# A decoder trunk's attention: rotating and transposing the queries one block ahead

## The chip, the cores and the metric

The kernel runs on one core of a Trainium2 chip. Its time is the device time of one execution in microseconds (us). Shown are the median, the lowest and the highest of three runs, and one further execution that the hardware profiler recorded; the rows of the trace come from that one.

## The reference

The reference is a trunk of two layers over one sequence of 512 tokens of width 1024. Each layer has a mixer of three head groups, which read one combined projection of the normalised input, and after it an MLP:

```python
for l in range(DEPTH):
    h = _rmsnorm(x, norm_mix_g[l])
    z = h @ w_in[l]
    q, k, v, qi, ki, wi, u5, z_ssd, xbc, dt_raw = _split(z, IN_SIZES)
    attn_out = _dsa_mixer(q, k, v, qi, ki, wi, ...)   # sparse attention, 8 heads of 64
    s5_out = _s5_mixer(u5, ...)                       # 16 groups of a complex diagonal scan
    ssd_out = _ssd_mixer(z_ssd, xbc, dt_raw, ...)     # Mamba-2, 4 heads of 64, chunks of 128
    mix = jnp.concatenate([attn_out, s5_out, ssd_out], axis=-1) @ w_out[l]
    x = x + mix
    h2 = _rmsnorm(x, norm_mlp_g[l])
    x = x + (jax.nn.relu(h2 @ w_up[l]) ** 2) @ w_down[l]
```

The attention goes over four blocks of 128 queries. Eight small index heads score every earlier token, and the 128 best of each query are kept. The queries and keys are normalised and the first 16 of their 64 elements are rotated by position; then comes softmax over the kept keys, and the sum of the values.

## The kernel before

**Streams and their merge.** One call of `mixers(l)` (L1382) does the mixer of a layer, as several Python generators: `trunk_in` (the input projection with its evacuations), `keys` (keys, then the index scores of blocks 1 to 3), `select` (the masks), `attention`, `recurrent` for S5 and for SSD, three parts of `out_proj`, and in layer 0 the tables of S5. `merge` (L1172) runs them in one another's gaps: each stream has a clock, the stream with the lowest clock takes its next step, and the number that the step yields is added to its clock. A step that yields None has to wait for another stream. The numbers are costs times a pace: `pace["q"]` is 3.616 in the first mixer and 3.741 in the second, so that the `pace["q"] * 2.5` after a query step is 9.04 and 9.35 units; a softmax of block b yields `pace["att"] * (0.4 + 0.25 * b)`, with 1.702 and 1.652. This fixes in which order the instructions are traced. The tile framework then orders them for each engine by priority and dependence; a stream's priority can be shifted (attention: 300 and 1000).

**Tiles.** Nearly all large tiles come from `g()` (L243), whose tag "g" has 52 buffers of 128 x 512 floats: weights have their own, but the queries, the head copies, the logits and their exponentials, the evacuated projections `xb` and `z` and, through `h()` (L247), SSD's tiles are all of it. Small tiles come from `s()` (L261) with a tag each. The PSUM banks are two pools, "m" and "a", of four banks each.

**Attention.** `attention` (L1341) waits until all four query blocks and the keys are there, computes the scale of each query head, and goes over the blocks. The step that this document calls a query step is in two parts. `rope_q` (L1033) rotates a block's queries with four VectorE operations on 16 elements of each head (L1038 to L1041), with a scratch tile `rsw` of its own tag. `transpose_heads` (L1071) then turns the eight heads so that the head's dimension lies on the partitions, in two halves of four heads each:

```python
t = self.g([P, 4, 2, 64], F32R, name="hhl")
nc.scalar.activation(t[:, :, 0], x, AF.Copy)                                    # L1078
nc.vector.tensor_tensor(t[:, :, 1], x, t[:, :, 0].bitcast(F32), ALU.subtract)   # L1079
p = self.ps(self.bank["hT"], (P, 4, P), name="hTp")
for i in range(4): nc.tensor.transpose(p[:, i], ...)                            # L1082
o = self.g([P, 4, P], F32R, name="hT")
nc.scalar.activation(o, p, AF.Copy)                                             # L1084
```

When the block's mask is there (block 0 has a constant one; `topk_masks` (L1116) makes the others, with the last write at L1126), `attend` (L1128) does the block: for each of eight heads the logits `lg` (TensorE, L1091), their masked maximum into `pe` (VectorE, L1143) and the exponential (ScalarE, L1144); the scaling by the reciprocal of the sum (L1151 and L1153); then for each block of keys the transposes `pTp` (L1159), their evacuation `pT` (ScalarE, L1161) and the product with the values into `po` (L1164); and the split of the result into `mh` and `ml` (L1168, L1169).

**Work beside it.** `trunk_in` evacuates the projections: `xb` at L1246 and `z` at L1249, both on VectorE. `ssd` (L828) makes from `xb` the convolution `cv` (L880 to L887) and the tiles `CT` (L893, L894), and then, chunk by chunk, the products `ssdT`, `ssds`, `ssdy` (L943, L945) with the VectorE work between them. `out_proj` (L1396) multiplies each group's `mh` and `ml` with the output weights as soon as they are complete (L458 to L460, which are the lines of every weight product).

Of the kernel before, what the change touches and what calls it, by code (L numbers as in the profile page):

```python
# [22 lines left out]
NB = S // P  # L23
# [197 lines left out]
class Net:  # L221
# [1119 lines left out]
    def attention(self, l, r):  # L1341
        nc = self.nc
        while len(r.get("q", ())) < NB or "K" not in r:
            yield None
        yield self.start["att"]
        q, rt = r["q"], self.rt
        qms = self.s([P, NB, NH], tag="qms", bufs=1)
        qrs = self.s([P, NB, NH], tag="qrs", bufs=1)
        for b in range(NB):
            self.head_ms(qms[:, b], q[b], NH)  # L1350
            yield self.pace["q"] * 0.7
        self.rsqrt(qrs.rearrange("p b h -> p (b h)"), qms.rearrange("p b h -> p (b h)"), NB * NH)
        nc.vector.tensor_scalar(qrs, qrs, -ATT_SCALE, None, ALU.mult)
        ah = [self.g(dt=F32R, name="mh") for _ in range(4)]
        al = [self.g(dt=F32R, name="ml") for _ in range(4)]
        for b in range(NB):
            self.rope_q(q[b], *rt[2][b])
            qT = self.transpose_heads(q[b])
            yield self.pace["q"] * 2.5
            while b not in r["mask"]:  # L1360
                yield None
            yield from self.attend(b, qT, r["K"], r["mask"][b], qrs[:, b], ah, al)
        for i in range(4):
            self.tap(f"at_{l}_{i}", ah[i].bitcast(F32)); self.tap(f"atl_{l}_{i}", al[i].bitcast(F32))
        r["mix"]["att"] = list(zip(ah, al))
# [252 lines left out]
```

## Time and profile before

| | us |
|---|---|
| median of 3 runs | 1325.63 |
| lowest and highest | 1324.28, 1325.82 |
| the profiled execution | 1325.5 |
| its span, first to last instruction | 1323.7 |
| TensorE busy (matmuls) | 1219.9 (92%) |
| VectorE busy | 888.7 (67%) |
| ScalarE busy | 548.9 (41%) |
| mean granted TensorE clock | 0.966 |

Engines are called PE (TensorE; PEld is its weight load), DVE (VectorE), ACT (ScalarE), POOL (GpSimd) and SP (SyncE). The profile gives the busy time of each, the idle time before an instruction with the instruction that ended it, and timelines; L1143 is a line of the kernel, and `pe<-lg,isc,qrs` names what is written and what is read. A row of a timeline has the start, the duration, the engine, the line and the operation; equal neighbours are one row with their count, such as x4. The first mixer's attention lies at 120 to 301 us of the span, the second's at 825 to 932 us; the MLPs fill most of the rest.

### The profile page before, as it was taken

Reading aid. Unit: us, or ns where it says so; the run is one execution under the profiler, and the core shown is the slowest. Engines: PE = TensorE matmul, PEld = TensorE weight load, DVE = VectorE, ACT = ScalarE, POOL = GpSimd, SP = SyncE. Lnnn points to the kernel's source line nnn. Section 1 sums busy time; section 2 is a strip of 40 time slices with the busy share of each in tenths; the row PEclk is TensorE's granted clock in tenths of the full one; section 3 lists DMA queues with packets and bytes.
Section 4 is the critical chain, followed back from the end, with each engine's and each line's share of the span. In section 5 each row is a group of like instructions: output and inputs, shape, how many; then the busy total and the mean of one; then the engine's idle time right before and its main releaser. Section 6 shows DMA issues by size and latency. Waiting matters only on the chain.

```text
span 1323.7 us, 17056 instructions
## 1 busy us (share of the span) xinstructions
PE 1219.9 (92%) x5708; PEld 979.0 (74%) x5708; DVE 888.7 (67%) x2024; ACT 548.9 (41%) x1128; POOL 172.8 (13%) x302
## 2 busy tenths in 40 slices
PE   5678967889999999999999988968999999999998
PEld 5566755458888888888888767744788888888887
DVE  5998999857877755554573699975475445445443
ACT  4245543663543533534443334455254243242331
POOL 2386100000599100000100000000000000000000
PEclk9789978899999999999999989978999999999999
DMA  5122320002467776686654634300323333333332
GB/s 190 40 80 65 81 81 9 24 1 71 130 196 253 230 252 217 218 266 199 211 171 145 204 120 129 112 17 1 111 89 103 96 96 96 96 99 99 97 111 80
DMA packets 139688, 161.64 MB, mean 122 GB/s; under 512 B 18768, under 2 KB 107600, under 8 KB 139600
## 3 DMA queue, kind: packets, MB, share of 16 engines
q1 hardware_dynamic: 139600, 160.55, 38.8%
q8 instruction: 45, 0.74, 0.2%
q14 instruction: 43, 0.35, 0.1%
HBM read 128.29 MB, written 31.03 MB: 120 GB/s over the span
## 4 chain that ended last, share of the span: by engine, by line
PE 74%; DVE 19%; ACT 4%; issue 2%; DMA 0%; SPq 0%; ACTq 0%; DVEq 0%
PE pm L458 21%; PE pm L460 21%; PE pm L459 21%; PE po L1164 3%; DVE isc L1123 2%; DVE mx L1122 2%; PE pTp L1159 1%; DVE isc L1112 1%; DVE pe L1143 1%; DVE cv L883 1%; ACT pe L1144 1%; PE hTp L1082 1%; DVE wlo L192 1%; DVE hhl L1079 0%; PE bct L428 0%
## 5 line engine op out<-in xcount | busy, mean ns | idle before, releaser
L192 DVE TENSOR_TENSOR wlo<-wraw,whi 128x512 fp32r<-128x512 f32 (+1 forms) x312 | 225.6, 726 | 230.5 <-ACT whi L191 224.2
L191 ACT ACTIVATE whi<-wraw 128x512 fp32r<-128x512 f32 (+1 forms) x312 | 194.5, 625 | 378.5 <-PE pm L459 252.0
L458 PE MATMUL pm<-xh,whi 128*128 128x512 f32 x640 | 252.7, 396 | 3.8 <-ACT q L1260 3.3
L460 PE MATMUL pm<-xh,wlo 128*128 128x512 f32 x640 | 250.9, 393 | 1.2 <-DVE wlo L192 1.2
L459 PE MATMUL pm<-xl,whi 128*128 128x512 f32 x640 | 251.4, 393 | 0.0
L458 PE MATMUL pm<-uh,whi 128*128 128x512 f32 x512 | 199.7, 390 | 0.0
L459 PE MATMUL pm<-ul,whi 128*128 128x512 f32 x512 | 199.2, 389 | 0.0
L460 PE MATMUL pm<-uh,wlo 128*128 128x512 f32 x512 | 198.9, 389 | 0.0
L458 PEld LDWEIGHTS pm<-xh,whi 128*128 128x128 f32 x640 | 121.2, 190 | 31.5 <-ACT q L1260 4.0
L460 PEld LDWEIGHTS pm<-xh,wlo 128*128 128x128 f32 x640 | 121.2, 189 | 27.2 <-DVE wlo L192 2.0
L459 PEld LDWEIGHTS pm<-xl,whi 128*128 128x128 f32 x640 | 121.3, 190 | 24.5 <-issue 0.2
L458 PEld LDWEIGHTS pm<-uh,whi 128*128 128x128 f32 x512 | 96.1, 188 | 20.0 <-issue 0.2
L460 PEld LDWEIGHTS pm<-uh,wlo 128*128 128x128 f32 x512 | 96.1, 188 | 19.9
L459 PEld LDWEIGHTS pm<-ul,whi 128*128 128x128 f32 x512 | 96.2, 188 | 19.9
L458 PE MATMUL pm<-whi,xh 128*128 128x512 f32 (+1 forms) x176 | 67.6, 386 | 13.8 <-ACT xh L392 12.8
L460 PE MATMUL pm<-whi,xl 128*128 128x512 f32 (+1 forms) x176 | 66.9, 382 | 1.1 <-DVE xl L394 1.1
L459 PE MATMUL pm<-wlo,xh 128*128 128x512 f32 (+1 forms) x176 | 67.5, 383 | 0.1
L1444 DVE TENSOR_TENSOR ul<-ur,uh 128x512 fp32r<-128x512 f32 x64 | 48.7, 762 | 20.7 <-ACT uh L1443 20.4
L1442 DVE SCALAR_TENSOR_TENSOR ur<-pm,ur 128x512 f32<-128x512 f32 x64 | 43.9, 685 | 26.5 <-ACT ur L1439 26.5
L1450 DVE TENSOR_TENSOR sq<-pm,r2b 128x512 f32<-128x512 f32 x64 | 44.1, 689 | 22.4 <-PE pm L460 22.3
L1443 ACT ACTIVATE uh<-ur 128x512 fp32r<-128x512 f32 x64 | 40.0, 625 | 30.5 <-DVE ur L1442 30.5
L1123 DVE MATCH_REPLACE8 isc<-mx,isc 128x256 f32<-128x256 f32 (+2 forms) x96 | 52.0, 546 | 0.0
(345 smaller groups left out, 1940.3 us busy)
## 6 DMA issues: line engine op xcount, KB each, us to landing
wraw<-in_w_up_dram SPq DMA_DIRECT2D x128, 256.0 KB, 2.8
wraw<-in_w_down_dram SPq DMA_DIRECT2D x128, 256.0 KB, 2.8
st<-shi SPq DMA_DIRECT2D x48, 256.0 KB, 2.8
st<-slo SPq DMA_DIRECT2D x48, 256.0 KB, 3.4
wlo<-st SPq DMA_DIRECT2D x48, 256.0 KB, 2.9
whi<-st SPq DMA_DIRECT2D x48, 256.0 KB, 2.8
wraw<-in_w_in_dram SPq DMA_DIRECT2D x32, 256.0 KB, 2.8
sraw<-in_w_in_dram SPq DMA_DIRECT2D x32, 256.0 KB, 3.4
```

The lines of the kernel that those rows point to most:

```text
L191: nc.scalar.activation(hi, raw, AF.Copy)
L192: nc.vector.tensor_tensor(lo, raw, hi.bitcast(F32), ALU.subtract)
L458: nc.tensor.matmul(p, lh, rh, start=first, stop=False)
L459: nc.tensor.matmul(p, lh, rl, start=False, stop=False)
L460: nc.tensor.matmul(p, ll, rh, start=False, stop=last)
L1122: v.max(m8, acc)
L1123: v.match_replace(acc, m8, acc, SENT)
L1164: nc.tensor.matmul(po[g_ * 64:g_ * 64 + 64], self.vt[:, kb, g_], pts[g_], start=kb == 0, stop=kb == b)
L1442: v.scalar_tensor_tensor(r, p, 0.0, r, ALU.max, ALU.mult)
L1443: nc.scalar.activation(h, r, AF.Copy)
L1444: v.tensor_tensor(lo, r, h.bitcast(F32), ALU.subtract)
L1450: v.tensor_tensor(t, d[1], rb, ALU.mult)
```

## The change

The loop over the blocks rotates and transposes two blocks ahead of the first attention, and then always one block ahead:

```diff
         al = [self.g(dt=F32R, name="ml") for _ in range(4)]
+        turned = {}
         for b in range(NB):
-            self.rope_q(q[b], *rt[2][b])
-            qT = self.transpose_heads(q[b])
-            yield self.pace["q"] * 2.5
+
+            for i in range(b, min(b + (2 if True else 1), NB)):
+                if i not in turned:
+                    self.rope_q(q[i], *rt[2][i])
+                    turned[i] = self.transpose_heads(q[i])
+                    yield self.pace["q"] * 2.5
+            qT = turned[b]
             while b not in r["mask"]:
                 yield None
             yield from self.attend(b, qT, r["K"], r["mask"][b], qrs[:, b], ah, al)
```

With T for a query step and A for an attention, the order in the code was T0 A0 T1 A1 T2 A2 T3 A3 and is now T0 T1 A0 T2 A1 T3 A2 A3. The pause in the merge after each step goes with it. It holds in both mixers.

## Rows read from the trace of the kernel before

**Rows 1.** The page: busy time, share of the span and instructions of each engine.
```profile
PE 1219.9 (92%) x5708; PEld 979.0 (74%) x5708; DVE 888.7 (67%) x2024; ACT 548.9 (41%) x1128; POOL 172.8 (13%) x302
```

**Rows 2.** Windows: length, busy us of PE, PEld, DVE, ACT, POOL; PE clock, DMA share, GB/s.
```profile
120.00:160.00 40.00, 38.27 (x184) 29.07 (x182) 39.87 (x123) 24.40 (x54) 6.11 (x10) 1.00 0.25 65
...
216.00:301.00 85.00, 72.67 (x362) 47.70 (x362) 64.33 (x180) 50.16 (x135) 0.00 (x0) 0.92 0.04 13
838.00:931.00 93.00, 75.76 (x376) 50.22 (x376) 64.52 (x191) 52.71 (x147) 0.00 (x0) 0.89 0.10 33
```

**Rows 3.** PE's waits, 216 to 301 us, then 838 to 931: us in all, times, longest.
```profile
PE hTp L1082 <- DVE hhl L1079: 3.0, 3, 1.3
...
PE ssds L929 <- DVE CT L894: 4.2, 1, 4.2
PE ssdT L916 <- DVE cv L887: 3.5, 1, 3.5
```

**Rows 4.** Timeline of ACT in mixer 1, block 1's query step.
```profile
220.57 0.63 ACT L191 ACTIVATE whi<-wraw 128x512 fp32r<-128x512 f32 x1 [6.46 <-PE pm L459]
...
226.65 0.40 ACT L1078 ACTIVATE hhl<-q 128x256 fp32r<-128x256 f32 x1
...
230.62 0.60 ACT L1084 ACTIVATE hT<-hTp 128x512 fp32r<-128x512 f32 x1 [1.27 <-PE hTp L1082]
```

**Rows 5.** Timeline of DVE in mixer 1, 214 to 232 us.
```profile
214.25 1.28 DVE L1249 SCALAR_TENSOR_TENSOR z<-pm,rb 128x512 f32<-128x512 f32 x2
...
223.00 0.69 DVE L894 SCALAR_TENSOR_TENSOR CT<-cth,cv 64x512 f32<-64x512 f32 x1
...
231.93 0.47 DVE L1143 CUSTOM_DVE_ANT_0 pe<-lg,isc,qrs 128x256 f32<-128x256 f32 x1
```

**Rows 6.** Timelines of ACT and DVE in mixer 1, block 3.
```profile
267.74 0.42 ACT L1078 ACTIVATE hhl<-q 128x256 fp32r<-128x256 f32 x1
...
270.39 0.42 DVE L1126 TENSOR_SCALAR isc<-isc 128x512 f32<-128x512 f32 x1
...
272.92 0.75 DVE L1143 CUSTOM_DVE_ANT_0 pe<-lg,isc,qrs 128x512 f32<-128x512 f32 x1
```

**Rows 7.** Timelines of ACT and DVE in mixer 2, block 3.
```profile
899.42 0.42 ACT L1078 ACTIVATE hhl<-q 128x256 fp32r<-128x256 f32 x1
...
906.58 0.74 DVE L1143 CUSTOM_DVE_ANT_0 pe<-lg,isc,qrs 128x512 f32<-128x512 f32 x1
```

**Rows 8.** Timeline of DVE in mixer 1, the last operation of the rotations.
```profile
130.92 0.28 DVE L1041 TENSOR_TENSOR q<-q,rsw 128x128 f32<-128x128 f32 x1
...
137.16 0.28 DVE L1041 TENSOR_TENSOR q<-q,rsw 128x128 f32<-128x128 f32 x1
```

**Rows 9.** Timelines of PE and DVE in mixer 2: the xb product's end, its first evacuation.
```profile
842.93 0.47 PE L460 MATMUL pm<-xh,wlo 128*128 128x512 f32 x1
...
863.77 0.68 DVE L1246 TENSOR_TENSOR xb<-pm,rb 128x512 f32<-128x512 f32 x1
```

**Rows 10.** Timeline of DVE in mixer 1, the last softmax of block 0.
```profile
187.32 0.36 DVE L1143 CUSTOM_DVE_ANT_0 pe<-lg,cons,qrs 128x128 f32<-128x128 f32 x1
187.59 0.10 DVE L1143 DVE_READ_ACCUMULATOR2_ANT nmax<- 128x1 f32 x1
```

**Rows 11.** Timelines of ACT and DVE in mixer 2, block 0 to block 1's first copy.
```profile
833.05 0.42 ACT L1078 ACTIVATE hhl<-q 128x256 fp32r<-128x256 f32 x1 [3.15 <-DVE q L1041]
...
838.73 0.35 DVE L1143 CUSTOM_DVE_ANT_0 pe<-lg,cons,qrs 128x128 f32<-128x128 f32 x1
...
850.98 0.41 ACT L1078 ACTIVATE hhl<-q 128x256 fp32r<-128x256 f32 x1
```

**Rows 12.** Timeline of PE in mixer 1: SSD's last product and the next projection.
```profile
298.08 0.38 PE L945 MATMUL ssdy<-cs,prev 128*64 128x128 f32 x2
298.39 0.74 PE L458 MATMUL pm<-mh,whi 128*128 128x512 f32 x2
```

## The prediction

> **What bounds the kernel now.** I read the page's busy table first. TensorE (PE) is busy for 92% of the span [rows 1], so time can be won only where PE stands idle. The windows show where that is. From 216 to 301 us (the attention stretch of mixer 1) PE is busy 72.67 of 85 us; from 838 to 931 us (the same stretch of mixer 2) 75.76 of 93 us [rows 2]. So 12.3 and 17.2 us of PE idle lie where the four attention blocks run one after another, and 29.6 us bounds any gain there. VectorE (DVE) is not full there: 64.3 of 85 and 64.5 of 93 us. In 120 to 160 us, where the first query step runs, PE has 38.27 of 40 us and DVE 39.87: nothing is to be had there.
>
> Next I read PE's waits in these two stretches. In mixer 1 the transposes wait 3.0 us in three places for DVE's half of the step that the change moves. In mixer 2 the two longest waits are for other work: 4.2 us for SSD's CT and 3.5 us for its convolution [rows 3].
>
> Then I followed one query step from its first copy to the first softmax, block 1 of mixer 1: first head copy at 226.65, second transposed copy (hT) at 230.62, first softmax at 231.93 [rows 4, 5]. That is a gap of 5.3 us in which attention makes no softmax. Block 3 has 5.2 us of it in mixer 1 (267.74 to 272.92) and 7.2 us in mixer 2 (899.42 to 906.58) [rows 6, 7]. These gaps are what the change aims at.
>
> But why does the step come so late? The rotation of all four blocks is done soon after 137.16 us [rows 8] (the first and the last of four stand there). Block 1's query has been ready since then, yet its head copy starts at 226.65, although ScalarE (ACT) stood idle for 6.46 us just before 220.57 [rows 4]. Neither data nor engine is missing. What holds it, as I read the code and the trace together: tiles with the tag "g" are first written in the order in which the code allocates them, so a tile that is late holds every later one. The rotation's scratch tile has its own tag and went early; the head copies are "g" tiles and did not. The same is seen in mixer 2: PE ended the xb product at 843.4, and its evacuation, a "g" tile again, came at 863.77 [rows 9]. I argue from this order in all that follows.
>
> **The change, part by part.** It adds and removes no instruction, and moves no DMA: per block four small DVE operations and, twice, an ACT copy (0.40 us), a DVE subtraction, four transposes and an ACT evacuation (0.60 us) [rows 4] move. No queue of SP or POOL is passed. The order was T0 A0 T1 A1 T2 A2 T3 A3 (T a query step, A an attention); it becomes T0 T1 A0 T2 A1 T3 A2 A3. So if tiles go in the code's order, a step still stands between A0 and A1 and between A1 and A2, only it serves the block after next. Only the gap between A2 and A3 goes, and one step more stands ahead of A0. The pause after each step (9.04 and 9.35 units of the merge's clock) moves too: A0, A1 and A2 are traced that much later against the other streams.
>
> *Mixer 1, T1 ahead of A0:* near 135 to 144 us, beside weight products that fill PE (38.27 of 40). Cost 0; without that cover 4.6 us, first copy to the end of the second hT (226.65 to 231.22) [rows 4].
>
> *Mixer 1, A0 traced later:* by the pace constants A0 now comes after the z product's evacuation (214.25) and after SSD's CT (to 223.69) [rows 5]. Today its softmaxes are long done: the last is at 187.32 [rows 10]. They leave a stretch in which DVE is nearly full, so CT comes about eight softmaxes (0.36 + 0.10 us) or 3.7 us earlier. A0 itself, first softmax to the next head copy, takes 12.25 us in mixer 2 (838.73 to 850.98) [rows 11]. Then 4.0 us to the second hT [rows 4]: 223.7 - 3.7 + 12.25 + 4.0 = 236.2 against 231.93, +4.3. Bounds: -1 if A0 stays where it is, +8 if CT does not come earlier. I take +4.3, by its own rows.
>
> *Mixer 1, A1 to A2:* T3 stands where T2 stood, but A2's first logits do not read it. At most the last hop goes (230.62 to 231.93, 1.3 us): -1.
>
> *Mixer 1, A2 to A3:* -5.2. But mask 3 is final only at 270.39 + 0.42 = 270.81, and A3 starts at 272.92 [rows 6]. With 4.3 - 1 - 5.2 = -1.9 it just fits; half a microsecond for a place in DVE's order leaves **-1.6** (range -5 to +5, the low end if the mask search finishes earlier too).
>
> *Mixer 2, T1 ahead of A0:* PE has products to do then, but attention's chain sets this stretch's end, so I count the step in full: +4.6 (0 to 5.7, the whole step 0 there, 833.05 to 838.73 [rows 11]).
>
> *Mixer 2, xb against A1:* A1 is traced later, so xb's evacuation and the convolution come ahead of about half of A1. That feeds SSD earlier, and the waits of 3.5 and 4.2 us [rows 3] can shrink. Bounds -7.7 (both go) and +4.6 (they push A1 back by as much as a query step); nearest to the waits that are seen, and only in part: -2.
>
> *Mixer 2, last hops twice:* -2. *A2 to A3:* the gap is 7.2 us, but the same instructions take 5.2 in mixer 1; the other 2 are SSD's and stay: -5.2. Mixer 2: 4.6 - 2 - 2 - 5.2 = **-4.6**.
>
> Sum -6.2 against the profiled execution's 1325.5 us (span 1323.7 and 1.8 around it; the median of the runs is 1325.63, so no correction): **1319.3 us**. A no-change result is all within 0.2%, 2.7 us, about what can be told apart here.
>
> **A rule that speaks against it.** What the rows show: the gap repeats at each block, with a free DVE. The Trainium skill, page Perfetto Trace Analysis, section Optimization Strategy, says that the same gap repeating on the engine that should be busy can mean that too few buffers are there for the next tile. By that rule four more live tiles of hhl and hT per block would make the gaps longer. The rows speak for an order rather than a shortage: the rotation, in a tag of its own, went ahead at once, and "g" has 52 buffers, of which I count at most 39 live from the code. No row here shows the occupancy itself.
>
> **Rivals.**
> (a) *Nothing changes.* SSD's output chain ends with attention's: its last product is at 298.08, and the next projection begins at 298.39 [rows 12]. The change doesn't move SSD's chain, and four steps stand in the code as before. For it: that row. Against it: SSD waits in the same queues, so a shorter attention lets it through. 1325.5.
> (b) *Slower.* The order holds A0 and A1 behind SSD's start. Mixer 1 takes its upper bound, +8 - 1 - 5.2 = +1.8; mixer 2 has xb at its upper bound, 4.6 + 4.6 - 2 - 5.2 = +2.0: 1329.3. It decides if A1's first softmax in mixer 1 is later than about 237. For it: CT's end at 223.69 with nothing of A0 done. Against: PE is idle there, and A0 could go faster than in mixer 2.
> (c) *Buffers run short*, the repeated gap being a shortage: each of the four remaining steps between blocks costs another round of 4.6 us instead of saving 1: 18.4 less the 5.2 won back between A2 and A3 is 13.2, so 1338.7.
> (d) *The order doesn't hold*, and all steps slip away beside other work: six gaps of 5.2 us and more, bounded by 29.6 us of PE idle; with half of that, -15: 1310.5. For it: this is what the data dependences allow. Against: the late head copies and the late evacuation [rows 4, 9].
>
> **How the numbers follow.** Forecast 0.45, (a) 0.20, (b) 0.20, (c) 0.05, (d) 0.10. The forecast's own range is 1313 to 1326, so some of its share falls within 0.2%. Faster: 0.38 of the forecast and (d), 0.48. Same: 0.07 of the forecast and (a), 0.27. Slower: (b) and (c), 0.25. The range takes in (d) and (b), 1309.5 to 1331, and leaves out (c) and the far ends.
>
> **What would show it.** Right: the first copy of block 1 near 135 us in mixer 1; head copies of block 2 still only after A0's last evacuation; no head copy between A2 and A3; A3's first softmax near 271 us, right behind its mask; in mixer 2 xb's evacuation before A1 ends, and PE's waits for the convolution and CT smaller. Wrong: if block 2's copies come right behind block 1's, the order doesn't hold and (d) is on; if A1 starts later than 237 us, (b); if A3 starts earlier but the projection still begins near 298.4, (a).

## The result, and the profile after

The changed kernel takes 1341.43 us (median of 4 runs, 1339.46 to 1342.22) against 1325.62 us of the kernel before, measured beside it: a ratio of 1.0124, with a 95% interval of 1.0111 to 1.0136. It is 1.2% slower, some 16 us, where I had forecast 1319.3 us. The profiled execution has a span of 1339.7 us at a mean granted clock of 0.961, against 1323.7 us at 0.966.

The profile's first table says that no work was added: PE has 5708 matmuls as before, is busy for 1224.0 us, against 1219.9 [rows 1], and its share falls to 91%.

```profile
PE 1224.0 (91%) x5708; PEld 980.9 (73%) x5708; DVE 891.8 (67%) x2024; ACT 550.6 (41%) x1128; POOL 176.1 (13%) x302
```

The loss is idle time of PE in the two attention stretches. These are the windows after that answer to the two stretches of [rows 2]; each is 7 to 9 us longer than it was.

```profile
216.00:310.00 94.00, 69.61 (x340) 43.61 (x338) 63.56 (x194) 52.57 (x148) 0.00 (x0) 0.85 0.04 12
847.00:947.00 100.00, 78.55 (x378) 51.41 (x377) 65.28 (x192) 52.55 (x147) 0.00 (x0) 0.85 0.11 31
```

PE is idle 24.4 us of the first and 21.5 us of the second, against 12.3 and 17.2 us before [rows 2]. To give each mixer its share, I take two rows of ACT that mark the same places in every kernel: the first evacuation of the queries (L1260), which comes before anything that the change touches, and the first evacuation of the last block's result (L1168). First the kernel before, then the changed one:

```profile
123.09 0.68 ACT L1260 ACTIVATE q<-pm,rstd 128x512 f32<-128x512 f32 x1
...
297.62 0.28 ACT L1168 ACTIVATE mh<-po 128x128 fp32r<-128x128 f32 x1 [0.64 <-PE po L1164]
...
825.43 0.66 ACT L1260 ACTIVATE q<-pm,rstd 128x512 f32<-128x512 f32 x1
...
931.37 0.28 ACT L1168 ACTIVATE mh<-po 128x128 fp32r<-128x128 f32 x1 [0.65 <-PE po L1164]
```

```profile
121.41 0.68 ACT L1260 ACTIVATE q<-pm,rstd 128x512 f32<-128x512 f32 x1
...
306.50 0.28 ACT L1168 ACTIVATE mh<-po 128x128 fp32r<-128x128 f32 x1 [0.64 <-PE po L1164]
...
834.64 0.67 ACT L1260 ACTIVATE q<-pm,rstd 128x512 f32<-128x512 f32 x1
...
947.31 0.28 ACT L1168 ACTIVATE mh<-po 128x128 fp32r<-128x128 f32 x1 [0.65 <-PE po L1164]
```

Mixer 1 went from 174.5 to 185.1 us, mixer 2 from 105.9 to 112.7 us. That is +10.6 and +6.7; with 1.7 us less ahead of the first row it is nearly the 16.0 us of the spans. One such length from one execution is good to some 2 us: in the six kernels of this document that have mixer 1 as it was, the one before among them, it lies between 174.4 and 176.7.

**Mixer 1 after.** Timelines of ACT (the head copies and hT) and of DVE (the rest), to be held against [rows 4, 5, 6, 10]:

```profile
217.21 0.69 DVE L894 SCALAR_TENSOR_TENSOR CT<-cth,cv 64x512 f32<-64x512 f32 x1
217.91 0.35 DVE L1143 CUSTOM_DVE_ANT_0 pe<-lg,cons,qrs 128x128 f32<-128x128 f32 x1
...
233.89 0.41 ACT L1078 ACTIVATE hhl<-q 128x256 fp32r<-128x256 f32 x1
...
239.91 0.60 ACT L1084 ACTIVATE hT<-hTp 128x512 fp32r<-128x512 f32 x1 [2.34 <-PE hTp L1082]
...
240.98 0.48 DVE L1143 CUSTOM_DVE_ANT_0 pe<-lg,isc,qrs 128x256 f32<-128x256 f32 x1
...
253.89 0.42 DVE L1126 TENSOR_SCALAR isc<-isc 128x512 f32<-128x512 f32 x1
...
279.44 0.74 DVE L1143 CUSTOM_DVE_ANT_0 pe<-lg,isc,qrs 128x512 f32<-128x512 f32 x1
```

Block 1's step is early (142.59), as the change says. But A0, whose softmaxes used to be done by 187.7 us [rows 10], begins only at 217.91, in the very slot behind CT; A1 begins 9 us late, and block 2's step before it takes 6.0 us from copy to hT instead of 4.0. The search for mask 3, in exchange, ends at 254.3 instead of 270.8 us [rows 6].

Two things are different in that step. DVE has a piece of the search (L1122) right ahead of its half of the first copies (L1079), and PE's clock is lower: four transposes take 1.1 instead of 0.6 us. Two rows of the step after; then the window of block 1's step before and that of the step after, with the length, the busy time of PE, PEld, DVE, ACT and POOL, and PE's granted clock:

```profile
234.46 0.68 DVE L1122 MAX8 mx<-isc 128x8 f32<-128x512 f32 x1
235.06 0.41 DVE L1079 TENSOR_TENSOR hhl<-q,hhl 128x256 fp32r<-128x256 f32 x1
```

```profile
226.60:231.20 4.60, 4.08 (x30) 3.55 (x28) 4.42 (x10) 1.93 (x6) 0.00 (x0) 1.00 0.12 39
...
233.90:240.50 6.60, 2.85 (x12) 2.46 (x13) 6.06 (x14) 1.89 (x5) 0.00 (x0) 0.50 0.11 38
```

**Mixer 2 after.** Timelines of DVE, with ACT's first evacuation of A2's result at 918.89:

```profile
871.42 0.48 DVE L1143 CUSTOM_DVE_ANT_0 pe<-lg,isc,qrs 128x256 f32<-128x256 f32 x1
...
871.83 0.69 DVE L1246 TENSOR_TENSOR xb<-pm,rb 128x512 f32<-128x512 f32 x1
...
882.05 0.35 DVE L1143 CUSTOM_DVE_ANT_0 pe<-lg,isc,qrs 128x256 f32<-128x256 f32 x1
...
898.50 0.62 DVE L1143 CUSTOM_DVE_ANT_0 pe<-lg,isc,qrs 128x384 f32<-128x384 f32 x1
...
918.89 0.28 ACT L1168 ACTIVATE mh<-po 128x128 fp32r<-128x128 f32 x1 [0.42 <-PE po L1164]
...
919.41 0.74 DVE L1143 CUSTOM_DVE_ANT_0 pe<-lg,isc,qrs 128x512 f32<-128x512 f32 x1
...
931.92 0.75 DVE L1143 CUSTOM_DVE_ANT_0 pe<-lg,isc,qrs 128x512 f32<-128x512 f32 x1
```

A1 is cut in two: after its fourth softmax (871.42) DVE does xb and the convolution, and the fifth comes at 882.05. The gap from A2 to A3 is gone (918.89 to 919.41), yet A3's eight softmaxes now need 12.5 us. PE's waits after, in 216 to 310 us and in 847 to 947 us:

```profile
PE hTp L1082 <- DVE hhl L1079: 12.1, 4, 5.2
...
PE ssdT L916 <- DVE cv L887: 5.1, 1, 5.1
PE ssdy L943 <- DVE dec L932: 4.5, 1, 4.5
...
PE ssds L929 <- DVE CT L894: 0.2, 1, 0.2
```

The wait for CT is all but gone (0.2 instead of 4.2 us [rows 3]). But the wait for the convolution has grown from 3.5 to 5.1 us, the wait for SSD's decay from 2.7 to 4.5 us, and PE waits 4.0 us, ending at 882.56, for the softmaxes of A1's second half.

### The profile page after: what moved, and what is told of

The parts are those of the page before. It is cut to its first block, busy times and chain, and to the rows that moved or that the text cites. A ratio compares the mean times of both kernels' runs of the same rounds, so it can differ in the third digit from the quotient of the medians.

```text
span 1339.7 us, 17040 instructions
## 1 busy us (share of the span) xinstructions
PE 1224.0 (91%) x5708; PEld 980.9 (73%) x5708; DVE 891.8 (67%) x2024; ACT 550.6 (41%) x1128; POOL 176.1 (13%) x302
## 4 chain that ended last, share of the span: by engine, by line
PE 74%; DVE 17%; ACT 4%; issue 2%; DMA 1%; POOL 0%; SPq 0%; ACTq 0%; DVEq 0%
PE pm L458 21%; PE pm L460 21%; PE pm L459 21%; PE po L1164 3%; DVE isc L1123 2%; DVE mx L1122 1%; PE pTp L1159 1%; DVE isc L1112 1%; ACT pe L1144 1%; DVE cv L883 1%; PE hTp L1082 1%; DVE pe L1143 1%; DMA wraw<-in_w_in_dram 1%; DVE wlo L192 1%; PE s5st L690 1%
## 5 line engine op out<-in xcount | busy, mean ns | idle before, releaser
L192 DVE TENSOR_TENSOR wlo<-wraw,whi 128x512 fp32r<-128x512 f32 (+1 forms) x312 | 228.4, 734 | 225.5 <-ACT whi L191 221.8
L1455 DVE TENSOR_TENSOR sq<-pm,r2b 128x512 f32<-128x512 f32 x64 | 44.1, 689 | 22.2 <-PE pm L460 21.9
L458 PE MATMUL pm<-mh,whi 128*128 128x512 f32 x128 | 50.9, 401 | 1.6 <-ACT mh L820 1.6
```

The lines of the kernel that those rows point to most:

```text
L192: nc.vector.tensor_tensor(lo, raw, hi.bitcast(F32), ALU.subtract)
L458: nc.tensor.matmul(p, lh, rh, start=first, stop=False)
L1455: v.tensor_tensor(t, d[1], rb, ALU.mult)
```

## The experiments

The change has two parts that can be told apart: the **order** of the steps, and the **pauses** that went with them and set where the merge puts each attention. Below, T and A are query steps and attentions as in the description of the change, and the lengths of the mixers are taken as above.

### Order alone, pauses alone, one mixer alone

*The order alone*: every block has one pause, at the place of before.

```diff
-            for i in range(b, min(b + (2 if True else 1), NB)):
+            for i in range(b, min(b + 2, NB)):
                 if i not in turned:
                     self.rope_q(q[i], *rt[2][i])
                     turned[i] = self.transpose_heads(q[i])
-                    yield self.pace["q"] * 2.5
+            yield self.pace["q"] * 2.5
             qT = turned[b]
```

> The query steps stand one block ahead, as in the changed kernel, but each block has its one pause where the kernel before has it, so that every attention is traced at the merge's clock of before. Theory P (place): the loss comes from the pauses, which put attention later against the other streams; then this one is at 1319 to 1329 us, A0's first softmax in mixer 1 is back near 145 to 150 us, and mixer 1 ends within 2 us of before. Theory S (step): the moved steps themselves cost it, by the tiles and banks that they take ahead of the next attention; then it stays at 1335 us or more, with A1 of mixer 1 still starting 5 us or more late.

*The pauses alone*: the kernel before with

```diff
-            yield self.pace["q"] * 2.5
+            for _ in range((2, 1, 1, 0)[b]):
+                yield self.pace["q"] * 2.5
```

> The query steps stand where the kernel before has them, right ahead of their own block; only the pauses are those of the changed kernel (two ahead of A0, one ahead of A1 and A2, none ahead of A3). P: 1335 to 1346 us, A0's first softmax in mixer 1 near 218 us as in the changed kernel. S: 1322 to 1330 us.

*One mixer alone*: in the changed kernel `2 if True else 1` became `2 if l == 0 else 1`, and then `2 if l == 1 else 1`.

> The change in mixer 1 alone. By the offsets of the two traces mixer 1 accounts for 9 us of the 16 and mixer 2 for 7: 1333 to 1336 us if the two are independent. Rival: mixer 2's loss is only a consequence of mixer 1's shift; then this is near 1341 us and the change in mixer 2 alone near 1326 us.

> The change in mixer 2 alone. Independent: 1331 to 1334 us, with the convolution of xb between the softmaxes of A1 and a PE wait for SSD's decay (dec) of over 4 us near A3. Rival: near 1326 us.

Measured, beside the kernel before on the same chip (1325.05 us):

| | us | ratio (95%) | mixer 1 | mixer 2 |
|---|---|---|---|---|
| before (profile above) | | | 174.5 | 105.9 |
| the change (profile above) | 1341.43 | 1.0124 (1.0111 to 1.0136) | 185.1 | 112.7 |
| order alone | 1331.93 | 1.0058 (1.0040 to 1.0076) | 174.5 | 114.6 |
| pauses alone | 1336.29 | 1.0091 (1.0070 to 1.0112) | 183.7 | 106.6 |
| mixer 1 alone | 1334.12 | 1.0073 (1.0055 to 1.0092) | 183.9 | 105.9 |
| mixer 2 alone | 1329.93 | 1.0044 (1.0028 to 1.0059) | 174.4 | 112.3 |

The rows of the first two experiments behind this table, with A0's first softmax in mixer 1 for the order alone; that one first, then mixer 1 of the pauses alone (its mixer 2 goes from 834.95 to 941.59):

```profile
121.64 0.68 ACT L1260 ACTIVATE q<-pm,rstd 128x512 f32<-128x512 f32 x1
...
147.91 0.34 DVE L1143 CUSTOM_DVE_ANT_0 pe<-lg,cons,qrs 128x128 f32<-128x128 f32 x1
...
296.09 0.28 ACT L1168 ACTIVATE mh<-po 128x128 fp32r<-128x128 f32 x1 [0.64 <-PE po L1164]
...
822.97 0.68 ACT L1260 ACTIVATE q<-pm,rstd 128x512 f32<-128x512 f32 x1
...
937.60 0.28 ACT L1168 ACTIVATE mh<-po 128x128 fp32r<-128x128 f32 x1 [0.64 <-PE po L1164]
```

```profile
122.86 0.68 ACT L1260 ACTIVATE q<-pm,rstd 128x512 f32<-128x512 f32 x1
...
306.57 0.28 ACT L1168 ACTIVATE mh<-po 128x128 fp32r<-128x128 f32 x1 [0.64 <-PE po L1164]
```

The order alone lies between the ranges of the two theories, and the pauses alone in that of P. So neither theory holds for the whole kernel; each holds for one mixer. In mixer 1 the loss is the pauses: with the order alone A0 is back at 147.91 and the mixer is as long as before, with the pauses alone it has +9.2 of the +10.6 us, and A0 begins at 217.90. In mixer 2 it is the order: +8.7 us alone, while the pauses alone do +0.7. (Both together do +6.7; that the pauses give 2 us back beside the order is no more than the lengths can tell.) The two mixers are nearly independent: each changed alone has the length that it has in the changed kernel, within 1.2 us, and the two times add up to 14 of the 16 us. Mixer 2 alone came out somewhat below its expectation, with the wait for the decay that it named (4.5 us).

### Mixer 1: is it A0 alone?

One pause more ahead of A0 and one less ahead of A1, in mixer 1 alone: `(2, 0, 1, 1)[b]` pauses instead of one each.

> Order of the steps as in the kernel before; in mixer 1 alone one pause more stands ahead of A0 and one less ahead of A1, so that only A0 is traced later (behind z and CT) and A1 to A3 stay at their old places in the merge. Theory F: mixer 1's whole loss is that A0 falls behind z and CT: A0's first softmax near 218 us, A1's near 240, mixer 1 ends 7 to 10 us late, 1331 to 1336 us. Rival: it needs the later pauses too; then mixer 1 ends within 3 us of before, 1322 to 1328 us.

It took 1327.38 us, a ratio of 1.0023 (1.0008 to 1.0038).

```profile
122.25 0.68 ACT L1260 ACTIVATE q<-pm,rstd 128x512 f32<-128x512 f32 x1
...
301.84 0.28 ACT L1168 ACTIVATE mh<-po 128x128 fp32r<-128x128 f32 x1 [0.65 <-PE po L1164]
```

A0 went where expected (217.53), but the mixer is 179.6 us long, +5.1 in this trace, and the time is only 2.5 us longer, which is within the rival's range. So A0's fall behind CT is half of what the pauses alone cost, or less (5.1 of 9.2 us by the traces, 2.5 of 11.2 by the times), and theory F, that it is all of it, was wrong. What the run with all the pauses has beyond this one is that A1 and A2 too are traced one pause later; they do the rest.

### Mixer 2: which moved step costs?

In mixer 2 only, with pauses as before, I moved one step at a time. *First*: T0 T1 A0 A1 T2 A2 T3 A3. *Last*: T0 A0 T1 A1 T2 T3 A2 A3. The diff is that of *first*; in *last* the four entries are (0,), (1,), (2, 3) and ().

```diff
-            for i in range(b, min(b + (2 if True else 1), NB)):
-                if i not in turned:
...
+            for i in (((0, 1), (), (2,), (3,))[b] if l else (b,)):
+                self.rope_q(q[i], *rt[2][i])
+                turned[i] = self.transpose_heads(q[i])
+            yield self.pace["q"] * 2.5
+            qT = turned[b]
```

> Mixer 2 only, pauses as in the kernel before: block 1's query step is moved ahead of A0, blocks 2 and 3 stay right ahead of their own attention (T0 T1 A0 A1 T2 A2 T3 A3). So as many steps stand ahead of xb's evacuation as before. Theory D (displacement): what the moved steps cost in mixer 2 is that one step more stands ahead of xb and SSD; then A0 starts 4 to 5 us late, the gap of A0 to A1 gives that back, xb is within 1.5 us of its place and the time is within 3 us of before (1322 to 1328). Rival: the step ahead of A0 costs by itself, since A0 then runs beside more of the output product; then xb and the end are 4 us late or more, 1329 or more.

> Mixer 2 only, pauses as before: only block 3's query step is moved, from ahead of A3 to ahead of A2 (T0 A0 T1 A1 T2 T3 A2 A3). My prediction's sum says +4.6 for the step and -5.2 for the gap: 1324 to 1326 us. Theory G (the gap of A2 to A3 is filled by SSD's work, which is taken back in A3): A3 starts near its old place or up to 2 us early against the mixer's start, and the mixer ends 2 to 5 us late: 1327 to 1331 us.

*First* took 1321.41 us against 1324.12, a ratio of 0.9991 (0.9970 to 1.0011): no difference that can be told. Its ten runs lie between 1319.1 and 1328.9, and the profiled one, at 1320.9, is among the short ones. DVE's rows, behind the first query evacuation at 824.61:

```profile
842.74 0.34 DVE L1143 CUSTOM_DVE_ANT_0 pe<-lg,cons,qrs 128x128 f32<-128x128 f32 x1
...
855.96 0.48 DVE L1143 CUSTOM_DVE_ANT_0 pe<-lg,isc,qrs 128x256 f32<-128x256 f32 x1
```

A0 starts 18.1 us behind that row instead of 13.3 (+4.8, the step); A1 31.4 instead of 30.8, and xb (862.67) 38.1 instead of 38.3 us. The gap that lost its step gave nearly all of it back, as theory D has it. In this kernel a step ahead of A0 did no harm where the next gap had none.

*Last* took 1327.2 us, 1.0017 (1.0008 to 1.0027), where my prediction's sum would have it at 1324 to 1326 and theory G at 1327 to 1331. A3 starts 81.3 us after the first row, as it did (81.2), and then the mixer ends 3.1 us late, as theory G has it. Why does A3 take longer? PE's timeline in the gap and in A3, first of the kernel before, then of *last*: SSD's `ssdT`, SSD's `ssdy` behind six of the logits, and the last of A3's logits.

```profile
901.73 0.52 PE L916 MATMUL ssdT<-cons,cv 128*128 128x128 f32 x3
...
911.50 0.45 PE L943 MATMUL ssdy<-dec,xd 128*64 128x128 f32 x4 [2.72 <-DVE dec L932]
...
914.31 0.63 PE L1091 MATMUL lg<-kl,hT 128*128 128x512 f32 x1
```

```profile
907.83 0.27 PE L916 MATMUL ssdT<-cons,cv 128*128 128x128 f32 x1
...
914.88 0.70 PE L943 MATMUL ssdy<-dec,xd 128*64 128x128 f32 x4 [3.88 <-DVE dec L932]
...
919.12 0.63 PE L1091 MATMUL lg<-kl,hT 128*128 128x512 f32 x1
```

In the kernel before, PE does the first products of SSD's next chunk (`ssdT`) while the query step fills the gap ahead of A3. Without the gap they stand among A3's logits, which begin at 906.54, and what is behind them comes later. A3's softmaxes take 12.4 us from first to last instead of 8.4. Of these 4.0 us, 1.2 are the longer wait for the decay (3.88 instead of 2.72 us), 1.4 lie behind it (4.2 instead of 2.8 us to the last logits, as all of `ssdy` stands there ahead of them and not a part), and the other 1.4 ahead of it, where the products of SSD's chunk are. That two logits stand behind `ssdy` and run at the lower clock (0.63 us) is no difference: they do so in the kernel before too.

### Does A3 wait for these two logits?

To take them from behind `ssdy` I put `ssdy` and `st` of mixer 2 into the other PSUM pool (`"dy": "m", "dst": "m"`), once with the last step moved and once in the kernel before.

> As the one that moves only block 3's step in mixer 2, and SSD's ssdy and st are put into PSUM pool m there. In its program two of A3's logits stand on PE right behind ssdy of SSD's chunk 2, and with the other pool they stand ahead of it. Theory W: A3 takes longer without the step ahead of it because these two logits wait behind ssdy, which waits for SSD's decay (dec), work that the gap had hidden. Then A3's softmaxes, 12.4 us from first to last in that run, take 9 us or less, and the mixer ends 2 us or more earlier than there, 1322 to 1326 us. Rival: SSD's own chain to its last chunk sets the end; then the softmaxes come early but the end stays, 1326 to 1329 us.

> The control: the kernel before with ssdy and st in pool m in mixer 2, the query steps in their old places. W: A3's softmaxes take 8.4 us from first to last in the kernel before, and lose their wait behind ssdy too; within 3 us of before, 1321 to 1326 us.

They took 1333.95 us, 1.0081 (1.0065 to 1.0096), and 1328.15 us, 1.0040 (1.0025 to 1.0056). Both lie above every range that was given for them. PE waits for the decay 1.0 us instead of 3.9, and A3's softmaxes take 6.0 us from first to last, as theory W has it. But the mixer didn't end earlier: it is 115.7 us long, against 109.1 with the last step moved alone. Rows of the first kernel, then of the control, in the gap from A2 to A3:

```profile
907.62 0.50 PE L1091 MATMUL lg<-kl,hT 128*128 128x512 f32 x1
...
912.55 0.42 DVE L919 TENSOR_TENSOR xd<-ssdT,dt 128x256 f32<-128x256 f32 x1 [1.26 <-PE ssdT L916]
...
914.01 0.75 DVE L1143 CUSTOM_DVE_ANT_0 pe<-lg,isc,qrs 128x512 f32<-128x512 f32 x1
```

```profile
905.57 0.39 PE L1091 MATMUL lg<-kl,hT 128*128 128x512 f32 x1
...
908.05 0.42 DVE L919 TENSOR_TENSOR xd<-ssdT,dt 128x256 f32<-128x256 f32 x1 [2.80 <-PE ssdT L916]
...
909.50 0.75 DVE L1143 CUSTOM_DVE_ANT_0 pe<-lg,isc,qrs 128x512 f32<-128x512 f32 x1
```

So a shorter wait shortened A3, but the time came back ahead of it. From A2's first evacuation (907.73) to A3's first softmax there are 6.3 us with no query step in them, and 7.5 us in the control that has one. The rows say what fills them. A3's first logits are done at 908.1 us, and in the control at 906.0, yet the first softmax comes 5.9 and 3.5 us later (0.6 in the kernel before): DVE does SSD's work on the next chunk first, and stands idle for its `ssdT`. With the other pool that work is ahead of A3's softmaxes in DVE's order, and that is most of the 4 us by which the control is slower. The experiment thus changed two things, and it doesn't decide between theory W and its rival. What it does show is that this gap can be SSD's as well as the query step's.

### What holds the steps back

The argument on the order of tiles was tried on the kernel before: the steps' tiles got a tag of their own, and with that in mixer 2 a PSUM pool without logits.

```diff
-GBUFS = {"g": 52, "t": 16}
+GBUFS = {"g": 44, "t": 16, "q": 8}
...
-            qT = self.transpose_heads(q[b])
+            qT = self.transpose_heads(q[b], "q")
```

> The kernel before with one thing changed: the attention's head copies and transposed queries are tiles of a tag of their own with 8 buffers, and the tag g has 44 instead of 52. Theory O (order of tiles): what holds a query step back is that tiles of one tag are first written in the order of the code; then the first half's copy of each block moves ahead of the block before's end (block 1's in mixer 1 near 138 us instead of 227), the second half still waits for the PSUM tiles, the gaps shrink by 1 to 3 us each, and the time is 1317 to 1325 us. Rival B (buffers): the gaps come from too few buffers in g; then 44 are worse than 52, 1328 us or more.

> As the one with an own tag, and in mixer 2 the transposes of the query step are put into the other PSUM pool (m), where no logits or attention transposes lie. O: in mixer 2 each query step now runs inside the attention of the block before, the gaps from the last evacuation to the next softmax fall from 5 to 8 us to about 2, and mixer 2 is 4 to 9 us shorter: 1315 to 1322 us. If the gaps are covered by SSD's work anyway (theory G: the gap is used, what it gives is taken back in the next attention), it is within 3 us of the one with an own tag alone.

The own tag took 1319.72 us against 1324.12, a ratio of 0.9978 (0.9962 to 0.9993): 0.2% less than before, within the 1317 to 1325 of theory O. Block 1's first copy in mixer 1 starts at 138.11 us, instead of 226.65; the copy of its other four heads still comes late, at 217.24:

```profile
138.11 0.46 ACT L1078 ACTIVATE hhl<-q 128x256 fp32r<-128x256 f32 x1
```

So the tag held the first copy. Was it the order in the tag, or a lack of free buffers? The eight of the new tag are kept for the step, so that its own copy can't tell. But with 44 buffers g's other tiles came no later than with 52: in mixer 1 `xb` starts at 144.47 us (144.42 before), `z` at 213.96 (214.25) and the last CT at 221.76 (223.00), with the mixer's first row at 123.13 (123.09). Had all 52 been taken in that time, 8 fewer should have held some of them back. So these rows speak against a shortage in g, and the order is what is left. What holds the other four heads, order or number of the PSUM tiles, no run of mixer 1 says. Nor is it shown where the gain lies: the profiled execution took 1325.3 us, the longest of the ten, and its mixers are 174.6 and 105.1 us long.

With the pool as well, the time was 1322.78 us, 0.9989 (0.9979 to 0.9999), no better, where theory O expected 1315 to 1322. There A1 starts 3.5 us behind A0's first evacuation (850.15 to 853.62), where the kernel before needs 8.1, but A0 itself takes longer, the next two gaps are not shorter (20.2 and 6.6 us from the first evacuation to the next softmax, 16.3 and 5.9 before), and mixer 2 is no shorter (109.1 us in its profile, again of the longest run). The gaps were not closed, so this is no test of what closing them would bring.

The own tag together with *first* took 1321.54 us, 0.9987 (0.9975 to 0.9999). The two ranges expected for it overlap there, so that it doesn't tell whether the two would add up.

> The own tag for the query step's tiles, and in mixer 2 block 1's step ahead of A0 (T0 T1 A0 A1 T2 A2 T3 A3, pauses as before). If the two add up (-3 and -1 us): 1319 to 1322 us. If the own tag already takes the first gap: as with the own tag alone, 1320 to 1323.

The kernel before with the own tag has the lowest ratio that I found, about 3 us; its ten runs lie between 1317.8 and 1325.3, and its interval overlaps with those of *first* and of the two together.

## Why the prediction was wrong

**What bounds it, and what holds a step back:** right. The loss is PE idle in the two stretches, and the own tag moved a copy from 226.65 to 138.11 us. As the order says, a step still stood between A0 and A1 and between A1 and A2. But the order in the tag is not all that holds a step: with the own tag the copy of block 1's other four heads still started at 217.24.

**Mixer 1, T1 ahead of A0, cost 0:** right. With the order alone A0 begins 26.3 us behind the mixer's first row instead of 21.1, and mixer 1 still has its old length.

**Mixer 1, A0 traced later, +4.3:** the mechanism was right and the size was not. This is the first step that failed. A1's first softmax came 9.1 us later, and 10.7 us against the mixer's first row. The sum had three terms: CT's end earlier by 3.7 us, 12.25 us from A0's first softmax to the next copy, and 4.0 us to the second hT. Measured were 5.8 (223.69 to 217.90; 4.1 against the mixer's first row), 16.0 (217.91 to 233.89) and 6.0 us (233.89 to 239.91). It also set a hT (236.2) against a softmax (231.93), as if the last hop were gone; it was still 1.1 us. I had taken A0's length from mixer 2, where the granted clock is 1.00 in A0 (838.7 to 851.0); behind CT it is 0.75 (217.0 to 230.6). I had taken the step's from 226.6 to 231.2, again at 1.00, and it ran at 0.50. DVE was as full in the step before as it is after; but now the search for mask 3, which moved up, stands in the step, right ahead of DVE's half of the copies. PE waits 12.1 us for DVE's halves in the two steps that are left, 7.3 of them ahead of A1, where it had waited 3.0 in all [rows 3]. How much of the longer A0 is the clock and how much is DVE's order, no run separates.

**Mixer 1, the rest, -1 and -5.2 down to the mask:** wrong in the sum. The gap of A2 to A3 did give 4.1 us: from A2's first softmax (262.23, and 251.63 before) to A3's it is 17.2 instead of 21.3 us. But it gave them to a stretch that was 10 us late, and A1 with the step behind it took 1.6 us more and A3 2.4 us more. With the order alone the gap gave nothing: A3 starts 21.6 us behind A2, at 273.73, right behind its mask, which was final only at 273.29. So the bound by the mask was real, but the mask itself came later, 151.7 us behind the mixer's first row instead of 147.7; I had taken its time as fixed. The pauses ahead of A1 and A2, which I had not priced at all, are half or more of what the pauses cost, as the run with the first pause alone says.

**Mixer 2, T1 ahead of A0, +4.6:** right, +4.9 in the change (A0's first softmax at 852.80, 18.2 us behind the mixer's first row instead of 13.3).

**Mixer 2, xb earlier (-2) and two last hops (-2):** wrong; measured -0.3 from A0's first softmax to A2's. xb did come ahead of half of A1, by 1 us against the mixer's start, and PE's wait for CT went (4.2 to 0.2 us). But its wait for the convolution grew from 3.5 to 5.1 us, and between A1's fourth and fifth softmax there are 10.6 us, and PE waits 4.0 us for the second four.

**Mixer 2, the gap of A2 to A3, -5.2:** this is the second step that failed, by its idea. I had taken 5.2 of the 7.2 us as the step's own, and 2 as SSD's. Between the first softmaxes of A2 and A3 only 1.0 us was saved (21.9 to 20.9), and A3 with its product then took 3.1 us longer (24.8 to 27.9). What the gap hid was SSD's next chunk; without the gap A3 waits for it. Moving that one step alone shows the same: the gap gave 3.4 us, A2 came 3.5 us later and A3 took 3.0 us more, and the time was 2.3 to 3 us longer.

**The sum for mixer 2:** 4.9 - 0.3 - 1.0 + 3.1 = +6.7, where I had -4.6.

**The rivals.** The slower one, in which A0 falls behind SSD's start, was the right place, and its sign held: A1 started at 240.98, past its 237. But its price, 1329.3, took the bound of +8 in mixer 1 and still subtracted the gaps in full. (a) was right about SSD, whose chain still ends with attention's (its last product at 306.96, the next projection at 307.27), and wrong to make it a tie. (c) gave the number that came nearest, 1338.7, and that is chance: its cause was too few buffers in g, and g's other tiles came no later with 8 buffers fewer. The rule of the Trainium skill's page Perfetto Trace Analysis (Optimization Strategy), that a repeating gap can mean too few buffers, was thus by these rows not the case here for g: with 8 buffers fewer in g and a tag of its own, the copy moved to 138.11 us. For the PSUM tiles it stays open. (d) did not come about: block 2's copies still came behind A0's evacuation, at 233.89.

## What to carry to other kernels

Where two chains of work interleave on the same engines, a gap in one is the other's time: before a gap is counted as gain, look at what the second chain does in it, and move one step alone to see whether the gap closes or only moves. And where a change carries a pace or a priority with it, time that part separately: here it cost more than the reordering itself. If a step must run early, it can be freed from the order that holds it (a tag of its own) before it is moved in the code: here the one gained 0.2% and the other lost 1.2%.

## What I had not expected of the hardware

In these traces a pause of PE can cost more than its length. In the run with the last step moved, the windows around the wait for the decay are these (PE's busy time is the second number, the granted clock the one after the five engines):

```profile
905.40:911.00 5.60, 5.50 (x35) 4.09 (x32) 4.53 (x15) 4.56 (x16) 0.00 (x0) 1.00 0.01 4
911.00:914.90 3.90, 0.02 (x3) 0.05 (x2) 3.90 (x12) 2.75 (x7) 0.00 (x0) 0.78 0.00 0
914.90:919.50 4.60, 4.60 (x22) 3.64 (x23) 2.44 (x7) 0.00 (x0) 0.00 (x0) 0.50 0.00 0
```

PE worked at 2.4 GHz (1.00) until 911.0, stood idle, and then did its next 4.6 us of work at 1.2 GHz (0.50). A 128x512 logit there takes 0.63 instead of 0.39 us, so I estimate from these rows that the wait of 3.9 us cost some 2 us more behind it (4.6 us x 0.24 / 0.63 is 1.8). The kernel before pays this too, behind its wait of 2.72 us (a granted clock of 0.62 from 911.5 to 916.0). In mixer 2 after the change the stretch behind the convolution, 882 to 892 us, has a granted clock of 0.56 in the same way, behind 10.2 us in which PE was busy for 1.64.
